# Loads moved to the planned SP queue, a transfer limit and a later landing in the planner, and a head that begins with 128 rows

## The chip, the cores and the metric

The kernel runs on one core of one Trainium2 chip. The number that counts is the device time of one execution in microseconds; of several runs the median is taken. A profiled execution gives the trace from which all rows below come; its span is counted from the first to the last instruction of the program.

The core has five engines that run their own instruction streams: TensorE (PE, matrix products; PEld is its weight load), VectorE (DVE), ScalarE (ACT), GpSimd (POOL) and SyncE (SP, which here only issues transfers). SP, ACT and POOL can each issue transfers (DMA); SP's and ACT's go to hardware queues, POOL's to a software queue. Streams are in order: an instruction that waits holds all behind it on its engine.

## The reference, cut to what matters

One transformer-like block for 256 tokens of width 2048, all in float32: a gated feed-forward network, a mixer, a second feed-forward network, each with a norm before and after and a residual.

```python
f = _swiglu(_rmsnorm(h, ln_ffn1_pre), ffn1_gate, ffn1_up, ffn1_down)   # 2048 -> 5632 -> 2048
h = h + 0.5 * _rmsnorm(f, ln_ffn1_post)
p = _rmsnorm(h, ln_mix_pre) @ w_in            # split into z_a, z_b, g_a, g_b
y_a = _rwkv7_branch(z_a, ...) @ w_proj_a      # a recurrence over the 256 tokens, 16 heads of 64
y_b = _pool_branch(z_b, ...) @ w_proj_b       # windowed means over 2, 4, 8, 16 tokens
mx = (sigmoid(g_a) * y_a + sigmoid(g_b) * y_b) @ w_out
h = h + _rmsnorm(mx, ln_mix_post)
f = _swiglu(_rmsnorm(h, ln_ffn2_pre), ffn2_gate, ffn2_up, ffn2_down)
h = h + 0.5 * _rmsnorm(f, ln_ffn2_post)
```

The weights (some 440 MB) are read from HBM once and each is used for 256 tokens only.

## The kernel before, in words

**Products.** Every float32 operand is split into two float32r parts H and L (`split`: ACT casts H, DVE subtracts to get L), and a product is three matmuls, H·H, H·L and L·H. A weight tile w of 128 x 1024 is loaded by SP (`get_w`), cast by ACT (wH) and subtracted by DVE (wL); there are five buffers for the raw tile and five for each part. Two column blocks (f and l) of 512 are made at a time, for the two halves of 128 tokens, in PSUM banks. Some groups of products go by a seven-product scheme (`Columns.early`, `late`, `quad`) that has fewer matmuls and more DVE work. The names l, f, mm and p in the profile are such PSUM banks.

**Activations turned.** The next product needs its input with features on the partitions. Where PE is not to do it by transposes (`transpose_split`: tr, then xH on ACT and xL on DVE), a block is *carried* (`carry_raw`): DVE transposes it in 32 x 32 squares (T1), SP writes it to a DRAM tensor (cx<-T) and reads it back in four transfers (x<-cx) that put the squares in place; then ACT casts xH and DVE subtracts xL. So the feed-forward networks carry each hidden column block, the mixer carries the inputs of the recurrence (those named in `Z_DMA`), of the pool branch and the first two column blocks of m (`MIX_DMA`).

**The head.** The first column block of ffn1_gate starts while x is still loading. `head` issues 16 idle transposes that keep PE at work (`WARM`), loads the norm weights g1 and x in eight pieces (h is the half of the tokens, c the column quarter) and the weight tiles in turn; `turn(h, c)` transposes a piece. Eight more idle transposes (`WARM2`) stand behind turn(1, 0), and the product for row block k follows for both halves, do(k, 0) and do(k, 1). The two first pieces of x are issued by ACT, the rest by SP. `normed` later makes normed copies of x (nx) for the seven-product scheme, and `setup_mixer` loads twelve small rows of mixer weights (cols) and transposes them; it is called through `s.after` behind the first column blocks.

**The ends of the stages.** `post` runs while the last product of each stage (`down`) is made: with column block 0 and 2 it loads 128 copies of the norm weights (gb, 512 KB), with block 2 `reload` loads the residual (four transfers of 512 KB: xr from x, h from the DRAM tensor hsp, which POOL wrote). In the mixer `pb_g` writes sigmoid(g_b)·y_b to DRAM (msp, by POOL), and `ev_pa` reads it back (mb, 512 KB for each of four column blocks), multiplies sga and adds. gb, xr, h and mb are all issued by POOL.

**The planner.** The order of each engine's instructions is written by a list scheduler in the kernel's own Python code (`Plan`). Each operation is recorded with a cost and a due time: PE's main stream goes in program order and its paces add up to a clock; another operation is due `lag` (12 us) after the clock at which it was recorded, or earlier if what uses it is due earlier. `simulate` then plays the program with these costs: an engine that is free takes, among the operations whose inputs, buffers and PSUM banks are there, the one due first. Operations other than PE's are taken at most `AHEAD` (40 us) before the clock of the main stream. A transfer is costed on one common line: it starts 1.9 us after its issue or when the line is free, takes its bytes, and has landed `LAND` (1.6 us) after. The recurrence is a stream of its own (chain) that goes ahead of the main one when its operands are ready.

`emit` writes the instructions of every engine in the planned order. On the chip the planned *times* bind nothing: an engine runs its stream as soon as semaphores (inputs, freed buffers) let it. A stream with little in it, like POOL's, can therefore run far ahead of the planned time. The framework gives SP's and ACT's transfers eight semaphores in turn, so a ninth waits until the first has landed; the planner before does not count that.

Nearly all rows of the profile have the same line, that of the recording helper (L477), so the names of tiles tell the steps apart.

Of the kernel before, what the change touches and what calls it, by code (L numbers as in the profile page):

```python
# [19 lines left out]
P = 128  # L20
# [61 lines left out]

SYNC = 55.0
LAND = 1600.0
SWITCH = 170.0
RUN = 16
COLD = 4800.0
# [6 lines left out]
class Plan:  # L94
# [188 lines left out]
    def simulate(s):  # L283
# [18 lines left out]
        events, now, done, dma, tab = [], 0.0, 0, 0.0, None  # L302
        out, rel = [], itertools.count()
        gate = {e: [] for e in engines}
        prog, cfg, held = 0.0, (0, 0), None

        def can(o):
            for i in o.new:
# [33 lines left out]
        def go(o):  # L342
            nonlocal done, dma, tab, prog, cfg
            e = o.eng
            if o.stream == "main" and e == "PE":
                prog = o.nom
            o.start = now
            for i in o.new:
                if i.slot is None:
                    i.slot = slots[i.tag].popleft()  # L350
                    turn[i.tag] += 1
            pace, dur = o.pace, o.dur
            if e == "PE":
                if o.cfg != cfg:
                    pace, dur = pace + SWITCH, dur + SWITCH
                cfg = o.cfg
            if o.tab and tab not in o.tab:
                tab = o.tab[0]
                pace, dur = pace + 1300, dur + 1300
            if e == "PE" and now < COLD:  # L360
                pace, dur = 2 * pace, dur + pace
            free[e] = now + pace
            if o.nbytes:
                dma = max(now + 1900, dma) + o.dur
                o.end = dma + LAND
            else:
                o.end = now + dur
            if e != "PE":
                for i in o.psum:
                    i.lock = e, o.end + SYNC  # L370
                    heapq.heappush(events, (o.end + SYNC, next(rel), None))
            done += 1
            out.append(o)
            heapq.heappush(events, (free[e], next(rel), None))
            for i in o.tiles:
                i.left -= 1
                i.dl = max(getattr(i, "dl", 0.0), o.end)
                if not i.left and i.tag in s.tags:
                    heapq.heappush(events, (i.dl + SYNC, next(rel), i))
            for x in o.succs:  # L380
                t = now if e == "PE" and x.eng == "PE" else o.end + SYNC
                if x.stream == "chain" and x.eng == "PE" and e != "PE":
                    t += 250
                x.ready = max(x.ready, t)
                x.left -= 1
                if not x.left:
                    heapq.heappush(wait[x.eng], (x.ready, x.i))
                    heapq.heappush(events, (x.ready, next(rel), None))
        while done < len(ops):
            moved = True  # L390
            while moved:
                moved = False
                for e in engines:
                    if free[e] > now:
                        continue
                    w, av = wait[e], avail[e]
                    while w and w[0][0] <= now:
                        _, i = heapq.heappop(w)
                        ready[i] = True
                        if e != "PE":  # L400
                            heapq.heappush(gate[e], (ops[i].nom, i))
                    g = gate[e]
                    while g and g[0][0] <= prog + AHEAD:
                        i = heapq.heappop(g)[1]
                        heapq.heappush(av, (ops[i].dl, i))
                    if e == "PE":
                        for st in rank:
                            q = streams[st]
                            if q and ready[q[0].i] and can(q[0]) and whole(q[0]):
                                held = q[0].run  # L410
                                go(q.popleft())
                                moved = True
                                break
                            if q and st == "chain" and cfg != (0, 0) and can(q[0]) and soon(q[0]):
                                break
                        continue
                    skipped = []
                    while av:
                        d, i = heapq.heappop(av)
                        if can(ops[i]):  # L420
                            go(ops[i])
                            moved = True
                            break
                        skipped.append((d, i))
                    for x in skipped:
                        heapq.heappush(av, x)
            if done == len(ops):
                break
            if not events:
                s.stuck(avail, streams, slots, turn, now)  # L430
                raise RuntimeError("plan is stuck")
            now = events[0][0]
            while events and events[0][0] <= now:
                _, _, i = heapq.heappop(events)
                if i:
                    slots[i.tag].append(i.slot)
# [54 lines left out]
class Block:  # L491
# [183 lines left out]
    def head(s, w, c0, KT, do, keep, xs):  # L675
        load, turn, square = xs
        w32 = {}

        def get(k, n):
            w32[k] = (n, s.get_w(w, k, n, c0, 512, own=True))  # L680

        def split(k):
            n, t = w32[k]
            keep(s.two(t, k, n, 512))
        ps = s.bank("warm")
        for _ in range(WARM):
            s.nc.tensor.transpose(ps[:, :P], s.ident, s.ident)
        load(None, None)
        load(0, 0)
        load(1, 0)  # L690
        for k in range(4):
            get(k, 1)
        for c in range(1, 4):
            load(0, c)
            get(4 * c, 2)
            load(1, c)
            get(4 * c + 2, 2)
        split(0)
        turn(0, 0)
        split(1)  # L700
        last = turn(1, 0)
        split(2)
        split(3)
        with s.set(behind=last):
            for _ in range(WARM2):
                s.nc.tensor.transpose(ps[:, :P], s.ident, s.ident)
        for k in range(KT):
            do(k, 0)
            last = do(k, 1)
            if k % 2 == 0 and k + 4 < KT:  # L710
                turn(k // 2 % 2, k // 4 + 1)
                split(k + 4)
            if k == SQ:
                late = last
        with s.set(behind=late):
            for c in range(4):
                for h in range(2):
                    square(h, c)
# [206 lines left out]
class Kernel(Block):  # L925
# [28 lines left out]
    def ffn(s, wg, wu, wd, uT, rs, gpost, resid, emit, reload, xs=None):  # L954
# [31 lines left out]
            return lambda h, ps: (pss[i].append(ps), h and ev("fl"[i], pss[i]))  # L986
        s.gemm_tok(wg, 0, at, NKD, hold(0), lead=True, xs=xs)
        s.gemm_tok(wu, 0, at, NKD, hold(1))
        while s.after:
            s.after.pop(0)()  # L990
        rb = s.rtmp("rsb")
        s.spread(rs, rb)
        su = []
# [5 lines left out]
                              s.psum if b % 2 else s.bank)  # L999
        for b in range(1, nb):  # L1000
            J = jobs[b]
            s.block_seq(J, jobs.get(b + 1), evac([1.0, 1.0] if b > 1 else rs, [], J.banks))
        s.down(wd, s.T_at(hT), NKF, s.post(gpost, 0.5, resid, emit, reload), hT, sm,
               DOWN_QUADS)
# [10 lines left out]
    def normed(s, uT, rb, su):  # L1015
# [4 lines left out]
        for i in range(len(uT)):  # L1020
            (uH, uL), (nH, nL) = uT[i], nT[i]
            x = s.unit((P, 4, S), F32, "nx")
            V.tensor_tensor(out=fl(x), in0=fl(uH).bitcast(F32), in1=fl(uL).bitcast(F32),
                            op=ALU.add)
            V.tensor_tensor(out=x, in0=x, in1=rb.unsqueeze(1).to_broadcast([P, 4, S]),
                            op=ALU.mult)
            s.split(fl(x), fl(nH), fl(nL))
# [54 lines left out]
    def post(s, gpost, fac, resid, emit, reload):  # L1082
# [17 lines left out]

        def ev(c, h, ps):
            if h == 0 and c % 2 == 0:
                nc.gpsimd.dma_start(out=gb[c // 2], in_=gpost[c * 512:c * 512 + 1024]
                                    .partition_broadcast(P))

            def scale():
# [196 lines left out]
    def mixer(s, prm, uT, rs, resid, emit, gpost, reload):  # L1303
# [106 lines left out]
        def ev_pa(c):  # L1410
            T1 = []

            def ev(h, ps):
                if h == 0:
                    mbs[c] = s.unit((P, 2, 512), F32, "mb")
                    nc.gpsimd.dma_start(out=mbs[c], in_=msp[c])
                sg = sga[c][:, h]
                nc.vector.tensor_tensor(out=sg, in0=ps, in1=sg, op=ALU.mult)
                nc.vector.tensor_tensor(out=sg, in0=sg, in1=mbs[c][:, h], op=ALU.add)
# [401 lines left out]
def kernel(tc, x, ln_ffn1_pre, ln_ffn1_post, ffn1_gate, ffn1_up, ffn1_down,  # L1821
# [11 lines left out]
    with ExitStack() as ctx:  # L1833
# [10 lines left out]

        def load(h, c):
            if h is None:
                with s.set(lag=-20000.0):
                    nc.sync.dma_start(out=gr, in_=ln_ffn1_pre[0].rearrange("(k p) -> k p", p=P))
                ps = s.psum("pg1")
                nc.tensor.transpose(ps[:, :16], gr, s.ident[:16, :16])  # L1850
                nc.vector.tensor_copy(g1, ps[:, :16])
                return
            (nc.sync if c else nc.scalar).dma_start(
                out=at_tok(xs)(h, c), in_=x[0, h * P:h * P + P, c * 512:c * 512 + 512])

        def turn(h, c):
            return s.transpose_split(at_tok(xs)(h, c), uT, c, h, g1)
# [4 lines left out]
        def load_to(dst, src):  # L1862
            def f():
                for h in range(2):
                    for c in range(2):
                        nc.gpsimd.dma_start(out=dst[h][c],
                                            in_=src(h)[:, c * 1024:c * 1024 + 1024])
            return f
        hsp = s.dram((2, 2, P, D), "hsp")

# [54 lines left out]
```

## Time and profile before

| | |
|---|---|
| median of 3 runs | 2033.16 us (2027.96 to 2033.72) |
| the profiled execution | 2032.8 us, its span 2031.1 us |
| PE busy | 2002.6 us, 9837 matmuls |
| DVE, ACT, POOL busy | 1744.9, 1185.6, 80.9 us |
| moved by DMA | 470.91 MB, mean 232 GB/s |

By time the stages are: the head to about 31 us, the first feed-forward network to about 700, the mixer to about 1330 (its two recurrences have their serial parts near 940 to 980 and 1136 to 1175; the four products with w_proj_a begin at 1189), the second network to 2022.8, and the last norm and store to 2031.1.

In a row of a timeline the numbers are start and length in us, then engine, operation, out<-in, shapes and count; in brackets stands how long the engine had been idle before it and what ended that. SPq, ACTq and POOLq are the issuing of transfers; a row may merge several. In a list of waits the three numbers are the total, the times and the longest.

### The profile page before, as it was taken

To read this page: it belongs to the slowest core of one execution; us is meant where nothing else is said; L and a number is where in the kernel's file an instruction comes from. 1 tells how busy PE (TensorE), PEld (TensorE's weight loads), DVE (VectorE), ACT (ScalarE), POOL (GpSimd) and SP (SyncE) were. 2 spreads that over 40 slices of the span, in tenths; PEclk is the share of its full clock that TensorE was granted. 3 is DMA by queue.
4 is the path that set the end of the run, shared out by engine and by line. 5 is a ranking of instruction groups with operands and counts; after the bars stand their busy time and mean duration, and the time that the engine had idled before them with its cause. 6 is when DMAs were issued, how large, how long until landed. Compare 5 with 4: busy or idle time off the path is not lost.

```text
span 2031.1 us, 28147 instructions
## 1 busy us (share of the span) xinstructions
PE 2002.6 (99%) x9837; PEld 1655.5 (82%) x9837; DVE 1744.9 (86%) x2278; ACT 1185.6 (58%) x1588; POOL 80.9 (4%) x148
## 2 busy tenths in 40 slices
PE   9999999999999999999999998999999999999998
PEld 7888888888888888887887786888888888788886
DVE  7989999999888758897868768898899999998885
ACT  7555656565555556864845444575556565655552
POOL 0000000000001110001200110010000000000000
PEclk9999999999999999999999998999999999999999
DMA  7688888887667686656575576657888888876674
GB/s 270 228 260 266 283 267 273 273 278 227 206 205 255 220 245 212 196 178 189 153 229 179 168 232 198 229 199 237 260 263 284 264 275 270 270 228 214 198 258 138
DMA packets 254855, 470.91 MB, mean 232 GB/s; under 512 B 20592, under 2 KB 43258, under 8 KB 254714
## 3 DMA queue, kind: packets, MB, share of 16 engines
q1 hardware_dynamic: 248537, 448.68, 68.5%
q0 software_dynamic: 5888, 19.93, 2.9%
q8 instruction: 77, 1.26, 0.3%
q10 hardware_dynamic: 288, 0.52, 0.1%
q14 instruction: 65, 0.52, 0.1%
HBM read 444.40 MB, written 24.64 MB: 231 GB/s over the span
## 4 chain that ended last, share of the span: by engine, by line
PE 68%; DVE 13%; DMA 8%; issue 5%; ACT 4%; SPq 1%; DVEq 0%; POOL 0%; ACTq 0%; POOLq 0%
PE l L477 23%; PE f L477 20%; PE mm L477 18%; DVE wL L477 6%; PE p L477 5%; DMA x<-cx 3%; DMA w<-in_ffn_gate_dram 3%; ACT wH L477 2%; DVE t L477 2%; SPq L477 1%; DMA w<-in_ffn_up_dram 1%; DVE w L477 1%; DMA w<-in_w_proj_a_dram 1%; DVE T L477 1%; PE tr L477 0%
## 5 line engine op out<-in xcount | busy, mean ns | idle before, releaser
L477 ACT CAST wH<-w 128x1024 fp32r<-128x1024 f32 (+2 forms) x722 | 748.2, 1047 | 625.9 <-PE mm L477 142.8
L477 DVE TENSOR_TENSOR wL<-w,wH 128x1024 fp32r<-128x1024 f32 (+2 forms) x722 | 864.6, 1211 | 162.3 <-ACT wH L477 158.5
L477 PE MATMUL l<-wL,xH 128*128 128x512 f32 x788 | 307.1, 390 | 0.0
L477 PE MATMUL l<-wH,xH 128*128 128x512 f32 x788 | 306.9, 389 | 0.0
L477 PE MATMUL l<-wH,xL 128*128 128x512 f32 x788 | 306.6, 389 | 0.0
L477 PE MATMUL f<-wL,xH 128*128 128x512 f32 x672 | 261.7, 389 | 0.2 <-DVE wL L477 0.2
L477 PE MATMUL f<-wH,xL 128*128 128x512 f32 x672 | 261.6, 389 | 0.0
L477 PE MATMUL f<-wH,xH 128*128 128x512 f32 x672 | 261.4, 389 | 0.0
L477 PE MATMUL mm<-wH,xH 128*128 128x512 f32 (+1 forms) x672 | 261.0, 388 | 0.0
L477 PE MATMUL mm<-wH,xL 128*128 128x512 f32 (+1 forms) x672 | 260.9, 388 | 0.0
L477 PE MATMUL mm<-wL,xH 128*128 128x512 f32 (+1 forms) x672 | 260.6, 388 | 0.1
L477 PEld LDWEIGHTS l<-wL,xH 128*128 128x128 f32 x788 | 147.9, 188 | 31.5 <-DVE wL L477 0.7
L477 PEld LDWEIGHTS l<-wH,xH 128*128 128x128 f32 x788 | 147.9, 188 | 30.6
L477 PEld LDWEIGHTS l<-wH,xL 128*128 128x128 f32 x788 | 147.9, 188 | 30.2
L477 DVE TENSOR_TENSOR t<-w,w 128x1024 f32<-128x1024 f32 (+1 forms) x156 | 158.5, 1016 | 16.1 <-DMA w<-in_ffn_down_dram 8.3
L477 PEld LDWEIGHTS f<-wL,xH 128*128 128x128 f32 x672 | 126.1, 188 | 27.0 <-DVE wL L477 0.7
L477 PEld LDWEIGHTS f<-wH,xH 128*128 128x128 f32 x672 | 126.2, 188 | 26.1
L477 PEld LDWEIGHTS f<-wH,xL 128*128 128x128 f32 x672 | 126.2, 188 | 26.1
L477 PEld LDWEIGHTS mm<-wH,xL 128*128 128x128 f32 x672 | 126.2, 188 | 25.0
L477 PEld LDWEIGHTS mm<-wL,xH 128*128 128x128 f32 x672 | 126.2, 188 | 25.0 <-DVE wL L477 0.5
L477 PEld LDWEIGHTS mm<-wH,xH 128*128 128x128 f32 x672 | 126.2, 188 | 24.5
L477 DVE TENSOR_TENSOR wL<-t,wH 128x1024 fp32r<-128x1024 f32 x96 | 116.8, 1217 | 5.5 <-ACT wH L477 5.1
(308 smaller groups left out, 2679.4 us busy)
## 6 DMA issues: line engine op xcount, KB each, us to landing
w<-in_w_in_dram SPq DMA_DIRECT2D x128, 512.0 KB
w<-in_ffn_up_dram SPq DMA_DIRECT2D x116, 512.0 KB
w<-in_ffn_gate_dram SPq DMA_DIRECT2D x114, 512.0 KB
w<-in_ffn_down_dram SPq DMA_DIRECT2D x112, 512.0 KB
w<-in_ffn_gate_dram SPq DMA_DIRECT2D x184, 256.0 KB
w<-in_ffn_up_dram SPq DMA_DIRECT2D x180, 256.0 KB
w<-in_ffn_down_dram SPq DMA_DIRECT2D x128, 256.0 KB
cx<-T SPq DMA_DIRECT2D x31, 512.0 KB
```

Source lines behind the costliest of these rows:

```text
L477: ins = o.fn(*[real(x) for x in o.a], **{n: real(x) for n, x in o.k.items()})
```

## The change

1. The planner counts eight transfers of SP and ACT at once (`LANES`): SP takes no further one while the eighth last has not landed. A transfer that depends on another transfer lands `CARRY`, 1.8 us, later.
2. gb, mb and the residual loads (xr, h) are issued by SP in place of POOL: 22 transfers.
3. The head: its loads get due times in the order in which they are written, and that order becomes g1, x(0,0), two weight tiles, x(1,0), two weight tiles, the rest as before. x(0,0) is split in two, one half from ACT and one from SP; x(1,0) goes to SP. The eight idle transposes stand behind turn(0, 0), and the products begin with do(0, 0), do(1, 0) for the first 128 rows; the other half follows.
4. `setup_mixer` is called before the third column block after the first, not behind the first. The first operation of `normed` stands behind the product of k = 11 in the head.

```diff
+LANES = 8
+CARRY = 1800.0
@@ simulate, go(o)
             if o.nbytes:
                 dma = max(now + 1900, dma) + o.dur
                 o.end = dma + LAND
+                if any(ops[q].nbytes for q in o.preds):
+                    o.end += CARRY
+                if e != "POOL":
+                    lanes.append(o.end)
+                    heapq.heappush(events, (o.end, next(rel), None))
@@ simulate, the choice of an engine's next operation
+                    if e == "SP" and len(lanes) >= LANES and lanes[-LANES] > now:
+                        continue
@@ head
-        load(None, None)
-        load(0, 0)
-        load(1, 0)
-        for k in range(4):
-            get(k, 1)
+        seq = itertools.count()
+
+        def first(fn, *a):
+            with s.set(lag=-30000.0 + 300 * next(seq)):
+                fn(*a)
+        first(load, None, None)
+        first(load, 0, 0)
+        first(get, 0, 1)
+        first(get, 1, 1)
+        first(load, 1, 0)
+        first(get, 2, 1)
+        first(get, 3, 1)
         for c in range(1, 4):
...
         split(0)
-        turn(0, 0)
-        split(1)
-        last = turn(1, 0)
-        split(2)
-        split(3)
+        last = turn(0, 0)
         with s.set(behind=last):
             for _ in range(WARM2):
                 s.nc.tensor.transpose(ps[:, :P], s.ident, s.ident)
+        do(0, 0)
+        split(1)
+        do(1, 0)
+        turn(1, 0)
+        do(0, 1)
+        split(2)
+        do(1, 1)
+        split(3)
         for k in range(KT):
-            do(k, 0)
-            last = do(k, 1)
+            if k > 1:
+                do(k, 0)
+                last = do(k, 1)
...
             if k == SQ:
-                late = last
+                s.late = late = last
@@ ffn
         s.gemm_tok(wu, 0, at, NKD, hold(1))
-        while s.after:
-            s.after.pop(0)()
...
         for b in range(1, nb):
             J = jobs[b]
+            while s.after and b == 3:
+                s.after.pop(0)()
@@ normed
-            V.tensor_tensor(out=fl(x), in0=fl(uH).bitcast(F32), in1=fl(uL).bitcast(F32),
-                            op=ALU.add)
+            with s.set(behind=s.late):
+                V.tensor_tensor(out=fl(x), in0=fl(uH).bitcast(F32), in1=fl(uL).bitcast(F32),
+                                op=ALU.add)
@@ post
-                nc.gpsimd.dma_start(out=gb[c // 2], in_=gpost[c * 512:c * 512 + 1024]
+                nc.sync.dma_start(out=gb[c // 2], in_=gpost[c * 512:c * 512 + 1024]
                                     .partition_broadcast(P))
@@ mixer, ev_pa
-                    nc.gpsimd.dma_start(out=mbs[c], in_=msp[c])
+                    nc.sync.dma_start(out=mbs[c], in_=msp[c])
@@ tile_block_kernel, load
-                with s.set(lag=-20000.0):
-                    nc.sync.dma_start(out=gr, in_=ln_ffn1_pre[0].rearrange("(k p) -> k p", p=P))
+                nc.sync.dma_start(out=gr, in_=ln_ffn1_pre[0].rearrange("(k p) -> k p", p=P))
...
-            (nc.sync if c else nc.scalar).dma_start(
-                out=at_tok(xs)(h, c), in_=x[0, h * P:h * P + P, c * 512:c * 512 + 512])
+            o = at_tok(xs)(h, c)
+            for q, e in ((0, nc.scalar), (1, nc.sync)) if h + c == 0 else ((None, nc.sync),):
+                b = slice(0, 512) if q is None else slice(q * 256, q * 256 + 256)
+                e.dma_start(out=o[:, b], in_=x[0, h * P:h * P + P, c * 512:c * 512 + 512][:, b])
@@ tile_block_kernel, load_to
-                        nc.gpsimd.dma_start(out=dst[h][c],
-                                            in_=src(h)[:, c * 1024:c * 1024 + 1024])
+                        nc.sync.dma_start(out=dst[h][c],
+                                          in_=src(h)[:, c * 1024:c * 1024 + 1024])
```

More of the change, by code (lines that the diff above doesn't have):

```diff
@@ L304, in simulate @@
         gate = {e: [] for e in engines}
-        prog, cfg, held = 0.0, (0, 0), None
+        prog, cfg, held, lanes = 0.0, (0, 0), None, []
         def can(o):
@@ L687, in head @@
             s.nc.tensor.transpose(ps[:, :P], s.ident, s.ident)
-        load(None, None)
-        load(0, 0)
-        load(1, 0)
-        for k in range(4):
-            get(k, 1)
+        seq = itertools.count()
[9 more added lines that the diff above has]
+        first(get, 3, 1)
         for c in range(1, 4):
[L694 to L697, printed above, removed]
+            first(load, 0, c)
+            first(get, 4 * c, 2)
+            first(load, 1, c)
+            first(get, 4 * c + 2, 2)
         split(0)
-        turn(0, 0)
-        split(1)
-        last = turn(1, 0)
-        split(2)
-        split(3)
+        last = turn(0, 0)
         with s.set(behind=last):
```

## The prediction

> **What bounds the kernel now.** The first view is the page's table of busy time, the second the share of the span that each engine has in the chain that ended last.
>
> ```profile
> span 2031.1 us, 28147 instructions
> PE 2002.6 (99%) x9837; PEld 1655.5 (82%) x9837; DVE 1744.9 (86%) x2278; ACT 1185.6 (58%) x1588; POOL 80.9 (4%) x148
> PE 68%; DVE 13%; DMA 8%; issue 5%; ACT 4%; SPq 1%; DVEq 0%; POOL 0%; ACTq 0%; POOLq 0%
> ```
>
> TensorE is busy for 2002.6 of 2031.1 us. The change alters no matrix product, so all that it can win lies in the 28.5 us of gaps, in matmuls that run slowly just after a gap, and in the lead and tail. The third view is PE's list of waits (total, times, longest), with one line of ACT's.
>
> ```profile
> PE tr L477 <- DVE sga L477: 8.5, 1, 8.5
> PE pS L477 <- ACT Z L477: 2.9, 1, 2.9
> PE tr L477 <- DMA x<-in_x_dram: 1.7, 1, 1.7
> PE l L477 <- DVE hL L477: 1.4, 2, 1.2
> PE pr L477 <- DMA cols<-in_pool_scale_dram: 0.5, 1, 0.5
> ACT xH L477 <- DMA x<-cx: 37.5, 21, 8.0
> ```
>
> Each of these waits of PE is touched by one part of the change. The first, second and fourth follow a carried block (x<-cx, a block written to DRAM and read back transposed), as is shown below; the third and fifth lie in the head. What a gap costs is read from windows (the number in brackets after PE busy is its instructions; then other engines, granted clock, DMA share, GB/s):
>
> ```profile
> 1210.00:1220.00 10.00, 10.00 (x46) 8.29 (x45) 5.39 (x8) 2.11 (x2) 0.61 (x2) 1.00 1.03 281
> 1220.00:1230.00 10.00, 3.96 (x18) 2.95 (x16) 5.78 (x7) 3.98 (x5) 0.00 (x0) 0.84 0.69 244
> 1230.00:1240.00 10.00, 7.58 (x28) 6.41 (x29) 8.16 (x12) 4.09 (x6) 0.00 (x0) 0.65 0.76 221
> 950.00:960.00 10.00, 9.30 (x138) 7.52 (x139) 5.08 (x11) 2.32 (x5) 1.58 (x4) 0.83 0.19 58
> ```
>
> An undisturbed window holds 46 matmuls of 512 columns. From 1220 to 1240 there are 46 where 92 would fit. Eight of them are transposes of 128 columns, for which I put half a product's 0.22 us each (an estimate), 0.9 together. The other 38 are 8.3 us of work, so 20 - 8.3 - 0.9 = 10.8 us are lost: the wait of 8.5 and some 2.3 of matmuls at a granted clock of 0.65.
>
> **Why the mixer's end stands.** The timelines of POOL, SP, ACT, DVE and PE there:
>
> ```profile
> 1202.64 0.53 POOL L477 DMA_DIRECT2D h<-hsp  x1 [12.42 <-DVE sga L477]
> 1203.53 0.34 SPq L477 DMA_DIRECT2D cx<-T  x1
> 1203.85 0.53 POOL L477 DMA_DIRECT2D h<-hsp  x1 [0.69 <-DVE T L477]
> 1208.99 2.17 SPq L477 DMA_DIRECT2D x<-cx  x4
> 1209.56 0.53 POOL L477 DMA_DIRECT2D h<-hsp  x1 [5.18 <-ACT wH L477]
> 1213.47 0.53 POOL L477 DMA_DIRECT2D gb<-in_ln_mix_post_dram  x1 [3.38 <-DVE sga L477]
> 1214.49 0.34 SPq L477 DMA_DIRECT2D cx<-T  x1
> 1223.53 1.14 ACT L477 CAST xH<-x 128x512 fp32r<-128x512 f32 x2 [7.96 <-DMA x<-cx]
> 1232.42 1.09 PE L477 MATMUL tr<-ident,sga 128*128 128x128 f32 x4 [8.47 <-DVE sga L477]
> 1647.35 5.31 DMA x<-cx
> ```
>
> The first mixed block is written at 1203.53, and its four reads are issued from 1208.99 to 1211.16. ACT takes them up at 1223.53, 12.4 us after the last issue, and has stood 7.96 us for it. An ordinary carried read (the chain's row at 1647.35) lands in 5.31 us, so this one is about 7.1 us late. Beside it POOL has issued three residual reads and a norm-weight row, 0.5 MB each: 2.1 MB at the 281 GB/s of the window above are 7.5 us. That fits the delay. POOL issues them this early because nothing but a free buffer holds its queue back; the code places them in w_out's second half, far behind. Everything planned behind the carried block on ACT and DVE then moves back, the products sga that PE wants to transpose among it.
>
> **The change part by part.**
>
> *Loads moved from POOL to SP.* The rows of all that moves (issuing queue, count, size, us to landing):
>
> ```profile
> h<-hsp POOLq DMA_DIRECT2D x8, 512.0 KB, 8.9
> gb<-in_ln_ffn_post_dram POOLq DMA_DIRECT2D x4, 512.0 KB, 6.9
> xr<-in_x_dram POOLq DMA_DIRECT2D x4, 512.0 KB, 10.0
> mb<-msp POOLq DMA_DIRECT2D x4, 512.0 KB, 3.8
> gb<-in_ln_mix_post_dram POOLq DMA_DIRECT2D x2, 512.0 KB, 8.1
> ```
>
> These are 22 transfers. SP pays an issue for each, 0.34 to 0.54 us by the rows above (one of four reads is 2.17/4), so some 10 us over the whole run in a queue that mostly waits for weight buffers: nothing on PE's path. The bytes stay. What changes is when: on SP they stand behind the weight loads that the plan puts first, so the 2.1 MB leave the stretch in which the first mixed block is read. Its read then lands near 1211.2 + 5.3 = 1216.5, and the 7.1 us are won. With the 1.8 us of the next part that is 8.9, more than the wait of 8.5. What is late next is the second mixed block, written at 1214.49. By the first one's spacing (5.5 to its reads, 2.2 to issue them, 5.3 to land, 2.4 to cast and subtract) it is ready at 1229.9. PE wants it after the last of four projection products, at 1244.4 now and 10.8 us earlier if the gap closes, 1233.6: 3.7 us to spare. Bounds: -10.8 (all of it) and -1.8 (the plan's shift alone). I take -10, near the upper end, because the row of an ordinary read and the bytes give the same 7 us.
>
> By the Trainium skill (DMA: Bandwidth & Descriptors, Issuing engines are not separate DMA queues), transfers from the scalar, sync and gpsimd queues end up on the same DMA engines and interleave, and another issuer saves only issue time. By that rule the move alone wins nothing and the wait would shrink by the plan's 1.8 us only; it is the second rival below.
>
> *Carried blocks planned 1.8 us later.* The reader's own view of tile x says how late they are, then two of the places:
>
> ```profile
>   DMA x<-cx: 44.1, 24
> 948.86 1.30 ACT L477 ACTIVATE mz<-x,cols 128x256 f32<-128x256 f32 x3 [3.97 <-DMA x<-cx]
> 1737.64 1.14 ACT L477 CAST xH<-x 128x512 fp32r<-128x512 f32 x2 [2.60 <-DMA x<-cx]
> ```
>
> 24 waits of 1.84 us on average: 1.8 added to the estimated landing puts other work ahead of the cast about as long as the engines stand now. At 948.86 ACT stands 3.97 us and the chain's copy Z behind it holds PE for 2.9, in the window where the clock is 0.83. With 1.8 less, 1.1 us of wait stay, and of the 1.7 us that a clock of 0.83 takes from 10 us some 0.7 go: -2.5. Bounds: -4.6 (wait and clock wholly) and +3 (the recurrence drawn in a worse order, once more the same wait). At 1737.64 the 2.60 become 0.8, and of PE's waits for hL (1.4 in all) I take -1.3; bounds -1.4 and 0. Elsewhere ACT's waits hold up nobody, since PE does not appear in the list for them: 0. The later landing delays the second recurrence, fed by carried blocks. Its last product and the first that reads its output:
>
> ```profile
> 1174.69 0.28 PE L477 MATMUL pg<-lgs,kH 128*128 128x256 f32 x1
> 1189.11 0.39 PE L477 MATMUL mm<-wH,yH 128*128 128x512 f32 x1
> ```
>
> 14.4 us lie between, five carried blocks at 1.8 are at most 9, so this costs nothing while the cover stands.
>
> *Eight transfers at once.* This only tells the plan what SP already does, so it removes no wait and its cost is an order of instructions. I take 0, with the re-drawn order priced below.
>
> *Head.* The rows of the start:
>
> ```profile
> 7.46 0.66 PE L477 MATMUL tr<-ident,x 128*128 128x128 f32 x4 [1.68 <-DMA x<-in_x_dram]
> 8.74 0.48 PE L477 MATMUL mm<-wH,xH 128*128 128x512 f32 x1
> 6.93 0.69 DVE L477 TENSOR_TENSOR wL<-w,wH 128x512 fp32r<-128x512 f32 x1 [0.15 <-ACT wH L477]
> 12.36 1.22 DVE L477 TENSOR_TENSOR nx<-xH,xL 128x1024 f32<-128x1024 f32 x1
> 20.00:30.00 10.00, 9.54 (x44) 7.52 (x42) 9.70 (x22) 8.64 (x20) 0.00 (x0) 1.00 0.63 240
> 18.86 0.38 SPq L477 DMA_DIRECT2D cols<-in_rwkv_mu_dram  x1
> 28.58 0.25 SPq L477 DMA_DIRECT2D cols<-in_rwkv_mu_dram  x1
> ```
>
> PE stands 1.68 us for the second 128 rows and begins the product at 8.74. The first rows' own operands are complete at 6.93 + 0.69 = 7.6. Beginning with them wins 8.74 - 7.6 = 1.1, and the shorter first load a little more: -1.3, bounds -2.5 (wait and lead both) and 0 (the loads of w and x set the pace anyway). Taking nx (1.22 us) out of a stretch in which DVE is 9.70 of 10 busy, and the twelve small loads that hold SP from 18.86 to 28.83, wins the gap of 0.46 in that window and the wait of 0.5 for cols: -1.0, bounds -1.7 and 0. At their new place in the third column block the same twelve hold SP again: the price in the head was 0.96, five prepared weight tiles of 2.7 us (12 matmuls at 10/46 us) cover 13 us of it, so +0.5, bounds 0 and +1.
>
> *A new order everywhere.* The plan's costs change, so all engines get another order. It can leave waits of its own where there were none: +2, bounds 0 and +6 (twice the recurrence's wait).
>
> Sum: -10 - 2.5 - 1.3 - 1.3 - 1.0 + 0.5 + 2 = -13.6. The profiled execution took 2032.8 us (its span of 2031.1 and 1.7 around it), 0.4 under the median of the three runs, 2033.16, whose spread is 5.8 us. 2032.8 - 13.6 gives **2019 us**. All lower bounds together (-10.8, -4.6, -1.4, -2.5, -1.7) give -21.0, so 2012.
>
> By the Trainium skill (TensorE: Matmul & The Clock Gate, The HAM clock gate), the array falls to half its clock after some 3.4 us without work and needs as long to come back. The granted 0.65 after the wait of 8.5 us agrees, and by that rule the part of 2.3 us goes whole or not at all with the wait.
>
> **The rivals.**
> 1. *SP stands where POOL stood* (slower). The reads of h waited on POOL for 12.42, 5.18 and 0.69 us for their buffers. If SP meets such a wait, the weights and the carried reads queue behind it. Up to 13 us of it is covered by the prepared tiles; beyond, each us is one of PE's. One load that stands 20 us at each of three residual places (7 over the cover, 21 in all), with the mixer's gap left as it is and 5.6 won elsewhere less 2: 2032.8 + 21 - 3.6 = 2050. It decides from about 13 us at one place. For it: the waits above. Against: on POOL they arose because it ran ahead of the plan; on SP the plan issues a load when its buffer is free, and PE keeps the plan's pace. Chance 0.10.
> 2. *The move wins nothing*: the 2.1 MB still meet the carried read, now in SP's own queue. Then the mixer's end gives 1.8 instead of 10: 2032.8 - 5.4 = 2027.4. For it: SP has idle time there and may take the loads as early. Against: they are needed only in w_out's second half, beyond the window the plan opens. Chance 0.12.
> 3. *The change does not do what it says*: gaps close and as many open. 2032, within 0.3%. For it: PE has only 28.5 us of gaps in 9837 instructions, any order makes some. Against: outside the mixer the old order has nearly none. Chance 0.08.
>
> **How the numbers follow.** The forecast has 0.70, with its own range 2012 to 2026. The range for 8 in 10 is 2012 to 2030: it takes in the second rival and leaves the first, and most of the third, outside. A measurement of this kernel tells about 0.3% (6 us) from no change, so faster means under 2027: the forecast and four tenths of the second rival, 0.75. Same: most of the second's rest and of the third, 0.13. Slower: the first rival and a little of the third, 0.12.
>
> **What would show it.** Right: PE's wait for sga under 2 us, the windows of the w_proj_a products at 46 matmuls, POOL without h, gb, xr and mb, the reads of h behind the second mixed block on SP; ACT's total for x<-cx at half of 37.5; the first product under 8 us. Wrong: a long SP wait for a buffer with a weight load behind it, cols holding PE in the third block, or PE waits of several us in the recurrence where it had 2.9.

## The result and the profile after

The changed kernel takes 2016.83 us (median of 4 runs, 2016.10 to 2017.81), the kernel before in the same set 2031.35 us (2027.96 to 2033.72). The ratio is 0.993 with a 95% interval of 0.9913 to 0.9947, so it is faster by 14.5 us, where 2019 was forecast. Run again in two later sets it took 2019.92 and 2018.04 us against 2031.16 and 2033.66 (ratios 0.9941, 0.9925 to 0.9958, and 0.9926, 0.9909 to 0.9942): the gain is 11 to 16 us.

The page's busy time and the engines' share of the chain, and then PE's list of waits (total, times, longest), of the changed kernel:

```profile
span 2014.4 us, 28103 instructions
PE 1998.3 (99%) x9837; PEld 1653.1 (82%) x9837; DVE 1743.5 (87%) x2278; ACT 1185.9 (59%) x1588; POOL 67.5 (3%) x126
...
PE 93%; DVE 3%; ACT 2%; issue 1%; DMA 1%; SPq 0%; POOL 0%; DVEq 0%; POOLq 0%; ACTq 0%
```

```profile
PE pk L486 <- DVE nb L486: 2.0, 1, 2.0
PE warm L486 <- POOL ident masks.py:199: 1.5, 1, 1.5
PE pSa L486 <- ACT us L486: 0.9, 1, 0.9
PE zT L486 <- ACT zt L486: 0.8, 1, 0.8
...
PE tr L486 <- DMA x<-in_x_dram: 0.3, 1, 0.3
```

In the chain DMA fell from 8% to 1% and DVE from 13% to 3%, and PE rose from 68% to 93%: more of the steps that ended last are PE's own work. The waits for sga (8.5), Z (2.9), hL (1.4) and cols (0.5) are gone and that for x is 0.3 in place of 1.7; pk <- nb is longer, 2.0 in place of 1.2. ACT's wait xH <- x<-cx, of which the prediction said half of 37.5, is 6.9 us here, and 21.1 and 18.5 us in the two later profiles of the same kernel.

The windows at the mixer's end (columns as in the prediction), then the timeline of SP there and a row of ACT's:

```profile
1200.00:1210.00 10.00, 10.00 (x46) 8.27 (x45) 7.42 (x10) 3.89 (x4) 0.00 (x0) 1.00 0.98 285
1210.00:1220.00 10.00, 10.00 (x48) 8.31 (x47) 9.77 (x12) 4.58 (x6) 0.00 (x0) 1.00 0.97 290
1220.00:1230.00 10.00, 10.00 (x48) 8.28 (x48) 9.70 (x15) 6.96 (x9) 0.00 (x0) 1.00 0.80 256
```

```profile
1198.96 0.34 SPq L486 DMA_DIRECT2D cx<-T  x1
...
1203.93 1.84 SPq L486 DMA_DIRECT2D x<-cx  x4
...
1256.85 0.90 SPq L486 DMA_DIRECT2D h<-hsp  x2
...
1259.35 1.17 SPq L486 DMA_DIRECT2D h<-hsp  x2
```

```profile
1210.27 1.14 ACT L486 CAST xH<-x 128x512 fp32r<-128x512 f32 x2
```

No window has fewer than 46 matmuls and the granted clock stays at 1.00. The first mixed block's reads are issued by 1205.77 and its cast runs from 1210.27 without a wait, 4.5 us later in place of 12.4. The residual reads (h) come at 1256.85, 50 us behind the read that they had stood beside. The DMA engines carry no less for that: 270 GB/s from 1195 to 1225, and 272 from 1200 to 1225 in the kernel before. But there 2.10 of the 6.81 MB came by POOL's queue, and here nothing does.

Where the time came from is read from five marks on PE, by the first transpose of a network's result (tr<-fg), the first product with w_proj_a (mm<-wH,yH) and the last product. Of the kernel before (its mark at 1189.11 stands in the prediction), then of the changed one:

```profile
693.07 0.60 PE L477 MATMUL tr<-ident,fg 128*128 128x128 f32 x4
...
1324.19 0.60 PE L477 MATMUL tr<-ident,fg 128*128 128x128 f32 x4
...
2022.41 0.39 PE L477 MATMUL l<-kH,xL 128*128 128x512 f32 x1
```

```profile
690.92 0.60 PE L486 MATMUL tr<-ident,fg 128*128 128x128 f32 x4
...
1184.60 0.39 PE L486 MATMUL mm<-wH,yH 128*128 128x512 f32 x1
...
1308.94 0.60 PE L486 MATMUL tr<-ident,fg 128*128 128x128 f32 x4
...
2004.91 0.39 PE L486 MATMUL l<-kH,xL 128*128 128x512 f32 x1
```

| stretch | before | after | gain |
|---|---|---|---|
| start to the first network's result (head in it) | 693.07 | 690.92 | 2.15 |
| to the first product with w_proj_a (recurrences) | 496.04 | 493.68 | 2.36 |
| to the mixer's result (its end) | 135.08 | 124.34 | 10.74 |
| to the last product (second network) | 698.22 | 695.97 | 2.25 |
| to the end of the span | 8.64 | 9.49 | -0.85 |

### The profile page after: what moved, and what is told of

Its sections match the earlier page's. It is cut to its first block, busy times and chain, and to the rows that moved or that the text cites. A ratio compares the mean times of both kernels' runs of the same rounds, so it can differ in the third digit from the quotient of the medians.

```text
span 2014.4 us, 28103 instructions
## 1 busy us (share of the span) xinstructions
PE 1998.3 (99%) x9837; PEld 1653.1 (82%) x9837; DVE 1743.5 (87%) x2278; ACT 1185.9 (59%) x1588; POOL 67.5 (3%) x126
## 4 chain that ended last, share of the span: by engine, by line
PE 93%; DVE 3%; ACT 2%; issue 1%; DMA 1%; SPq 0%; POOL 0%; DVEq 0%; POOLq 0%; ACTq 0%
PE l L486 33%; PE f L486 29%; PE mm L486 22%; PE p L486 5%; DVE wL L486 1%; ACT wH L486 1%; PE tr L486 1%; DMA x<-cx 1%; PE pY L486 0%; DMA x<-in_x_dram 0%; DVE xL L486 0%; PE pSa L486 0%; PE pU L486 0%; PE pg L486 0%; ACT X L486 0%
## 5 line engine op out<-in xcount | busy, mean ns | idle before, releaser
L486 PEld LDWEIGHTS f<-wL,xH 128*128 128x128 f32 x672 | 126.2, 188 | 26.8 <-DVE wL L486 0.6
L486 PEld LDWEIGHTS f<-wH,xH 128*128 128x128 f32 x672 | 126.2, 188 | 26.1
L486 PEld LDWEIGHTS f<-wH,xL 128*128 128x128 f32 x672 | 126.2, 188 | 26.1
L486 PEld LDWEIGHTS mm<-wH,xL 128*128 128x128 f32 x672 | 126.2, 188 | 25.1
L486 PEld LDWEIGHTS mm<-wH,xH 128*128 128x128 f32 x672 | 126.2, 188 | 24.9 <-ACT zt L486 0.6
L486 PEld LDWEIGHTS mm<-wL,xH 128*128 128x128 f32 x672 | 126.2, 188 | 24.3
```

What stands on the lines that cost most here:

```text
L486: ins = o.fn(*[real(x) for x in o.a], **{n: real(x) for n, x in o.k.items()})
```

## The experiments

The theory: POOL's loads ran far ahead of the plan into the stretch in which a mixed block is read back, and the block came late; moving them in time gives the 10 us at the mixer's end, the later planned landing a few us in the recurrences and networks, the head 1 to 2. The main rival: the later planned landing closes the gap by itself. "Mixer's end" below is the third stretch of the table; each kernel's is taken between the same two marks.

### The 22 loads back on POOL

```diff
 changed kernel, in post, ev_pa and load_to:
-nc.sync.dma_start(
+nc.gpsimd.dma_start(
```

> The changed kernel with its 22 residual, norm-weight and pool loads back on POOL; planner constants and head as changed. Theory (the loads ran ahead on POOL into the read of the first mixed block): the wait of PE for sga comes back, 8.5 less the 1.8 of the later planned landing, so 6 to 7 us and 2 of slow clock behind it: about 2025 us (2023 to 2028). Rival (the later planned landing alone closed the gap): wait under 2 us, 2017 to 2019.

2026.38 us (2022.90 to 2028.06), ratio to before 0.9961 (0.9945 to 0.9977). Mixer's end 134.8 us. PE's wait, and ACT's timeline there:

```profile
PE tr L486 <- DVE sga L486: 8.3, 1, 8.3
```

```profile
1210.54 1.05 ACT L486 CAST wH<-w 128x1024 fp32r<-128x1024 f32 x1 [2.41 <-DMA w<-in_w_proj_a_dram]
1221.06 1.14 ACT L486 CAST xH<-x 128x512 fp32r<-128x512 f32 x2 [9.46 <-DMA x<-cx]
1222.10 2.93 ACT L486 CAST wH<-w 128x1024 fp32r<-128x1024 f32 x3
```

The gap is back, and not shorter by 1.8 as expected. The cast of the mixed block stands ahead of the same three weight casts as in the kernel before, and the order is unaltered; its wait of 9.46 us is 1.5 longer than the 7.96 there. The total lies in the expected range. A shift of 1.8 us is less than the 2.7 us from one cast of a weight to the next, which may be why it passed none of them.

### The 22 loads to SP, nothing else

```diff
 kernel before, in post, ev_pa and load_to:
-nc.gpsimd.dma_start(
+nc.sync.dma_start(
```

> The kernel before with the 22 loads moved to SP and nothing else. Theory: the mixer's end gives some 10 us, the recurrence, the head and the second network nothing: 2031.4 - 10 = 2021 (2019 to 2024), wait for sga under 2 us. Rival (later landing did it): 2030 to 2033 with the wait at 8 us. Rival (SP blocks where POOL waited): over 2033.

2024.60 us (2019.42 to 2027.92), ratio 0.996 (0.9942 to 0.9977). Mixer's end 125.7. PE's longest waits:

```profile
PE l L477 <- DVE hL L477: 3.1, 3, 1.2
PE pS L477 <- ACT Z L477: 2.0, 1, 2.0
...
PE tr L477 <- DVE sga L477: 1.1, 2, 0.8
```

The move alone closes the gap: 9.4 us of the mixer's end. The total gained less than the 10 expected, 8.4 against the 2033.01 of its set. In the profile the first network was 1.8 us longer and the second 1.5. PE's waits for hL grew from 1.4 to 3.1, and the carried blocks are as late as before (ACT stood 47.8 us for them, 44.1 before). How much of the shortfall is that and how much spread is not shown: the ten runs lie from 2019.42 to 2027.92, and the profiled one is among the longest, 2026.91.

### The later landing alone

```diff
 kernel before, in Plan.simulate:
                 o.end = dma + LAND
+                if any(ops[q].nbytes for q in o.preds):
+                    o.end += CARRY
```

> The kernel before with the carried blocks planned to land 1.8 us later and nothing else. Theory: wait for sga 6 to 7 us, wait in the recurrence 1 to 2, second network's 1.4 gone: 2031.4 - 5 = 2026 (2023 to 2029). Rival (later landing did it): wait for sga under 2 us, 2017 to 2021.

2026.66 us (2025.96 to 2030.05), ratio 0.9965 (0.9951 to 0.998). Mixer's end 134.3, with this wait of PE:

```profile
PE tr L480 <- DVE sga L480: 7.9, 1, 7.9
```

The rival falls: the later landing took 0.6 us from the wait and 0.8 from the stretch. The recurrences' stretch was 1.8 shorter (494.24), the second network 2.2 (695.97), and ACT's standing for carried blocks fell from 44.1 to 19.3 us. In all it gained 6.4 us against the 2033.01 of the set.

### POOL's residual reads held back by data

```diff
 kernel before, load_to, for the mixer's four reads alone:
+nc.gpsimd.tensor_copy(dst[h][c][:, :1], mT[3][0][:, 0, :1].bitcast(F32))
 nc.gpsimd.dma_start(out=dst[h][c], ...)
```

> The kernel before, the mixer's four residual reads still on POOL, but each preceded by a POOL copy of one column from the last quarter of m, so that they cannot run before the first mixed block is read. Theory (it is the time of the loads that matters, not the queue): wait for sga under 3 us (one norm-weight row still stands in the stretch), 2031.4 - 9 = 2022 (2020 to 2025). Rival (the kind of queue matters): wait stays near 8, 2030 to 2033.

2024.08 us (2017.64 to 2027.64), ratio 0.9947 (0.9929 to 0.9964). Mixer's end 126.2. POOL's and ACT's timelines, and PE's wait:

```profile
1243.25 3.67 POOL L477 COPY h<-xH 128x1 f32<-128x1 f32 x2 [61.15 <-ACT xH L477]
1247.21 0.54 POOL L477 DMA_DIRECT2D h<-hsp  x1 [0.29 <-POOL h L477]
...
1249.22 1.57 POOL L477 DMA_DIRECT2D h<-hsp  x3
```

```profile
1221.00 1.15 ACT L477 CAST xH<-x 128x512 fp32r<-128x512 f32 x2 [1.93 <-DMA x<-cx]
```

```profile
PE tr L477 <- DVE sga L477: 1.7, 1, 1.7
```

The reads are still POOL's, but run 45 us later, and 8.9 us of the mixer's end are gone. The held queue also took the second norm-weight row with it, so the share of the reads and that of the row are not told apart; the loads of mb stayed where they were. So the time of the loads matters and not the queue from which they come. The total spread over 10 us, and the profiled run, 2025.90, is among the longer; its recurrences took 498.58 us, 2.5 more than before, with the clock at 0.83 in two windows (830 to 840 and 950 to 960) where the kernel before had one. By the Trainium skill (DMA: Bandwidth & Descriptors, Issuing engines are not separate DMA queues) the issuing engine is no way to win bandwidth, since all transfers share the same DMA engines. The 126.2 from POOL beside 125.7 from SP agree. That moving them wins nothing does not follow, for a queue also decides when a transfer starts.

### No later landing in the changed kernel

```diff
-CARRY = 1800.0
+CARRY = 0.0
```

> The changed kernel with CARRY at 0. Theory (the loads' time closed the mixer's end; the later landing serves the recurrence and the feed-forward carries): mixer's end stays at 124 to 126 us, the recurrence's part is 2 to 3 us longer, ACT's waits for x<-cx go from 10 back to 20 us or more, waits of PE for hL return in the networks: 2020 (2018 to 2022). Rival (the later landing is worth nothing once the loads are out of the way): 2016 to 2017.5.

2023.10 us (2020.95 to 2026.04), 3.2 over the changed kernel in the same set (2019.92; the expectations call the unaltered changed kernel of a set the yardstick). Mixer's end 126.2, the recurrences 1.8 us longer (495.17). From the list of PE's waits, and the standing for tile x:

```profile
PE pS L486 <- ACT Z L486: 1.9, 1, 1.9
PE tr L486 <- DVE sga L486: 1.5, 2, 0.9
```

```profile
  DMA x<-cx: 39.6, 24
```

The recurrence's wait for Z is back, and some of that for sga; tile x is waited for 39.6 us in place of 25.5 in the set's changed kernel. So the later landing serves the recurrence, as expected. The networks do not bear the theory out: no wait for hL returns, and the second network takes 695.97 us, no longer than with the later landing. The loss was 1 us over the upper end, and the profiled run is the shortest of the four, 1.4 over its counterpart; the rest is in no profile.

### No count of eight transfers

```diff
-LANES = 8
+LANES = 10 ** 6
```

> The changed kernel without the count of eight transfers in the plan. Theory (it only tells the plan what happens anyway): 2016 to 2018.5, every stage within 1 us of the changed kernel's. Rival (without it the plan issues loads in an order that SP can't keep): over 2019, with SP's waits for landings longer and PE waits in the networks.

2018.67 us (2018.44 to 2020.66), 1.2 under the 2019.92 of the set. All stretches lie within 0.9 us of that kernel's. The count buys nothing that shows.

### The old head

The functions `head` and `load` as in the kernel before, with `s.late` kept; all else as changed.

> The changed kernel with the old head: old order of loads, the idle transposes behind turn(1, 0), both halves of each row block together. Theory: the products begin 1.0 to 1.5 us later and all that follows is moved by that: 2018 (2017 to 2019.5). Rival (loads set the head's pace, the order is worth nothing): 2016 to 2017.

2018.00 us (2016.99 to 2020.17), 1.9 under the 2019.92 of the set, with overlapping runs. Its start on PE and the first window:

```profile
7.18 0.70 PE L486 MATMUL tr<-ident,x 128*128 128x128 f32 x4 [1.82 <-DMA x<-in_x_dram]
7.67 1.91 PE L486 MATMUL warm<-ident 128*128 128x128 f32 x8
9.24 0.78 PE L486 MATMUL mm<-wH,xH 128*128 128x512 f32 x1
```

```profile
0.00:10.00 10.00, 6.72 (x35) 6.28 (x36) 2.77 (x8) 4.36 (x10) 0.75 (x7) 0.88 0.78 261
```

The product begins at 9.24, against 6.55 with the new head in this set. By the tile table of f, the second column block begins at 56.8 against 54.7, 2.1 us later. At the first network's result 1.0 of it is left (693.42 against 692.45), and 0.2 before w_proj_a: the lead is given back. So the new head wins 2 us for 50 us, and nothing that shows at the end, as the rival had it. The later place of the small loads and of nx is kept in this run: what they are worth, no run shows apart.

### The late block told to the plan

```diff
 loads on POOL as in the first experiment, and in ev_pa:
-                    s.carry(T1[0], mT, c)
+                    with s.set(slip=7000.0):     # added to the planned landing
+                        s.carry(T1[0], mT, c)
```

> As the changed kernel with the 22 loads back on POOL, but the plan is told that the two mixed blocks land another 7 us later. Theory (what costs is that the plan does not know of the late block, so that the cast stands ahead of work which is ready): the cast moves behind that work, PE's wait for sga falls from 8.3 to under 3 us although POOL's loads still collide with the read; mixer's end 125 to 128 us in place of 134.8, total 1 to 3 us over the yardstick. Rival (the bytes themselves hold up PE, through late weights or through m being late for w_out): PE waits of 6 us or more stay in this stretch, total as with the loads on POOL, 6 us or more over the yardstick.

2025.57 us (2023.74 to 2027.70), 7.5 over the changed kernel's 2018.04 in the set. Mixer's end 131.2: 3.6 us less than without the telling, 6.9 more than with the loads moved, and outside the 125 to 128 expected. PE's waits and a window:

```profile
PE tr L488 <- DVE sga L488: 2.2, 1, 2.2
...
PE f L488 <- ACT xH L488: 1.1, 1, 1.1
```

```profile
1230.00:1240.00 10.00, 6.31 (x20) 4.34 (x20) 10.00 (x16) 4.72 (x7) 0.00 (x0) 0.66 0.45 162
```

Both views are half right. Told of the late block, the plan puts ready work ahead of it and the wait for sga falls from 8.3 to 2.2. But now DVE is busy for all of 10 us with what had been put off, PE waits for the mixed blocks themselves, and the clock falls to 0.66. Here order could not hide all of the late block.

### The recurrence's small weights, and then all of POOL's transfers, on SP

```diff
 changed kernel, fill_l and fill_g; the second kernel also msp and hsp:
-G.dma_start(
+nc.sync.dma_start(
```

> The changed kernel with the recurrence's small weights (w2, a2, g2) loaded by SP too. Theory (the same mechanism: these loads run beside the read of a carried block near 940 us, where ACT stood 4.45 us): ACT's wait there under 2 us, the part before w_proj_a 1 to 2 us shorter than the yardstick's 493.5, total 1 to 2 us under the yardstick. Rival (msp and the plain landing time make it late, not these): no change within 1 us.

> As the one before, and the stores of msp and hsp from SP too, so that POOL issues no transfer. Theory: as the one before within 1 us. Rival (SP stands for results of DVE at the ends of the stages, and weights queue behind): 2 us or more over it, with PE waits after the first network's and the mixer's last columns.

2018.27 us (2017.44 to 2018.44) and 2016.47 us (2014.65 to 2018.46), beside 2018.04 for the changed kernel in the set: the first no change, the second 1.6 less with overlapping runs, so no clear gain. In the first, the standing of ACT near 945 us is gone, but because the operations that stood there come 29 us later in the new order (981.43 for 952.22), so whether the read would land sooner is not shown. And the small weights now queue behind SP's others. ACT's timeline and PE's waits:

```profile
828.64 1.04 ACT L486 CAST kH<-w 128x1024 fp32r<-128x1024 f32 x1 [2.68 <-DMA w<-in_rwkv_a_dram]
```

```profile
PE pw L486 <- ACT kH L486: 1.6, 1, 1.6
...
PE pw L486 <- DVE kL L486: 0.6, 1, 0.6
```

POOL had loaded them at 719 us, a hundred before their use. The stretch before w_proj_a was expected to be 1 to 2 us shorter and is 1.0 longer, 495.3 us against 494.2 in the set's changed kernel: the move won ACT's wait at one end of the recurrence and lost 2.2 us of PE's at the other.

### The changed kernel again

> The changed kernel unaltered, as the yardstick of this set: 2015 to 2018 us, with no wait for sga and 124 us between the first product with w_proj_a and the first transpose of the mixer's result.

> The changed kernel unaltered, yardstick of this set: 2016 to 2021 us, stages as before (wait for sga under 1 us, 124 to 125 us from the first product with w_proj_a to the first transpose of the mixer's result).

2019.92 us (2019.56 to 2021.03) and 2018.04 us (2016.75 to 2019.37); the mixer's end 124.9 and 124.3. The first is 1.9 us over the upper end of its expectation.

## Why the prediction was right, point by point

- **The mixer's end, -10 (10.74 measured).** The mechanism is shown from four sides: with the loads early on POOL the stretch is 134.3 to 135.1 us in three kernels (131.2 where the plan is told of it), with the loads on SP or held 124.3 to 126.2 in all others. That the whole gap closes, the clock's 2.3 us with it, was right. In the changed kernel the second mixed block holds up PE in none of its three profiles (ACT casts it at 1222.25 without a wait, and stands 0.81 us for it at most). But the working had 3.7 us to spare there, and they were not: in the two kernels with the loads on SP and no later landing ACT stands 1.91 and 2.07 us for the second block, and PE 0.77 and 0.92 behind it. The 1.8 us that the later landing was to add, and that were the second rival's price, came only in part: 0.3 and 0.8 us while the loads stay on POOL, and 1.3 once they are on SP (126.2 without it, 124.9 with it in the same set).
- **The recurrence, -2.5 (2.36).** The constant does it: 1.8 us alone, and 1.8 lost without it. But the size is right by other terms than those of the sum, which is luck. The working had a wait for Z of 1.1 us left over and 0.7 us of clock won. In fact the whole wait of 2.9 is gone and the low clock behind it too: from 950 to 960 it is 0.83 in all four kernels without the later landing, where PE waits 1.9 to 2.9 us for Z, and 1.00 in all ten profiles with it. That is the bound of -4.6. In return some 2.4 us of new waits came into the stretch (pk <- nb, pSa <- us and three short ones), so that PE's waits in it sum to 4.9 us in place of 5.4. ACT still stands for the block, and longer:

```profile
946.23 0.37 ACT L486 COPY Z<-pSa 64x256 f32<-64x256 f32 x1 [1.42 <-DVE Z L486]
...
952.22 1.31 ACT L486 ACTIVATE mz<-x,cols 128x256 f32<-128x256 f32 x3 [4.45 <-DMA x<-cx]
```

  The row is 4.45 where 3.97 stood (4.07 and 2.15 in the two later profiles), and PE's wait for Z is gone from the list all the same. The working had it that the wait itself shrinks by 1.8; it was the order, since the copy Z now goes ahead of the block. The copy us still stands behind it, and PE's new wait of 0.9 is for that.
- **The networks' carried blocks, -1.3 (2.25 in the second network; 0.6 and 1.4 in the two later profiles).** Met in size, but the later landing is not shown as its cause. The stretch is 696.0 to 697.7 us in the nine other profiles with it, but also 696.0 in two of the kernels without it (the held reads, and the changed kernel without the constant), 698.2 before and 699.7 with the loads on SP alone. The unaltered changed kernel alone has 696.0, 697.7 and 696.9, so most of this is spread, and the rest the new orders.
- **The head, -1.3 and -1.0, and +0.5 for the small loads (together 2.15 at the first network's result).** The sum is met in this execution (0.6 and 2.5 in the two later ones), but the first term is the step that fell: the bound of 0 that was given with it is what the experiment shows at the end of the program. Of the second, the signs are there: the window from 20 to 30 has PE at 10.00 in place of 9.54, and the wait for cols is gone. The small loads at their new place took 13.4 us on SP, among weight loads, and held PE nowhere:

```profile
114.98 0.46 SPq L486 DMA_DIRECT2D cols<-in_rwkv_mu_dram  x1
...
128.15 0.25 SPq L486 DMA_DIRECT2D cols<-in_rwkv_mu_dram  x1
```

- **A new order everywhere, +2.** In the profile it is 0.85 at the tail and the 2.4 us of new waits in the recurrences. Of these pk <- nb goes from 1.2 to 2.0 with the later landing alone too. The tail is 8.6 us in all five kernels with the loads early on POOL or held there, and 9.1 to 9.6 in seven profiles with them on SP; yet it is 8.5 to 8.6 in the two that have the small weights on SP as well. Its cause stays open.
- **The rivals.** SP never stood where POOL had stood: the move alone is 8.4 us faster. "The move wins nothing" is refuted by the second experiment, "the change does not do what it says" by the first three.
- **Two readings in the working.** Twelve matmuls at 10/46 us are 2.6 us and not 2.7, which is the distance of ACT's weight casts; five of either cover 13 us. And the wait for Z lies mostly before the window with the clock of 0.83: it ends at 950.70, and the low clock follows it.

By its range (2012 to 2030), its direction and the mechanism of its largest term the prediction holds; the 2019 lie 2.2 us from the first set's median and inside the spread of the three. From profile to profile the gain is 16.7 us where the sum has 13.6.

## What to carry to other kernels

A planned order binds only within one queue: in this kernel an engine with little to do ran its transfers as soon as their buffers were free, and they took their share of a busy DMA from a read that others waited for. Look for it where a transfer lands later than its like, at all queues' issues beside it, and move the early loads behind it, by a busier queue or by data that they wait for. A planner's landing time is worth matching to the mean wait in the trace (1.84 us here). It gained 6.4 us alone, and 3.2 us were lost without it, beside 8.4 for the move alone; the intervals of the two alone overlap, so which is worth more is not shown. But it does not replace removing what makes a transfer late: at the mixer's end it gained 0.8 us, the move 9.4.

## What was not expected of the hardware

The clock falls after less idle time than the kernel before had suggested. A wait of 1.68 us left it at 1.00 there (eight idle transposes in 1.04 us); with the old head a wait of 1.82 us left it lower, the eight took 1.91 us and the first window was granted 0.88. And with waits of 2.2 and 1.1 us close together the window had 0.66, where 0.65 followed the wait of 8.5. Nor does the length alone decide it. PE's wait pk <- nb is 1.99 us in all three profiles of the unaltered changed kernel. From 1015 to 1020 and from 1020 to 1025, around its end, the clock is 1.00 and 1.00 in two of them and 0.82 and 0.84 in the third, which takes up to 1.7 us from the ten. So the same wait cost nothing more in two executions and up to nearly its own length again in the third; what decides is not shown. As a least idle time for the clock to fall, the 3.4 us without work that the prediction names do not hold in these runs.

An unaltered kernel moved by 3 us between sets (2016.83, 2019.92, 2018.04), of which the first network, with the same order of instructions, made 2 in the profiles (683.99, 685.90 and 684.38 us from the first product to the first tr<-fg). An edit worth 1 or 2 us can't be told from that.
